# A two-layer streaming encoder step on one core: queue loads held behind older stores, weight splits at one step each, a first tile outside the pinned order, and all eight late key projections beside the first attention

## The chip, the cores and the metric

The kernel runs on one core of one Trainium2 chip. The time is the device time in microseconds (us) of one execution. The core's engines are named as the profile names them: PE (TensorE, matrix products; PEld is its weight load), DVE (VectorE), ACT (ScalarE), POOL (GpSimd) and SP (SyncE, which here only issues DMAs, one after the other). Each engine works through its own instructions in order and waits on semaphores for the others. Three runs of the kernel before took 3301.7, 3307.01 and 3307.56 us, a median of 3307.01 us.

## The reference

One step of a two-layer encoder over 2048 prompt frames and 64 sample frames, 16 heads of 64. Layer A is a softmax attention over a band of chunks, layer B a stick-breaking attention over all earlier frames; both multiply their output by a SiLU gate, project it and add it to the residual stream. Cut to what is computed:

```
def gated_out(o, gate, w_out):
    return (o.reshape(b, t, D_MODEL) * jax.nn.silu(gate)) @ w_out

def band_attend(q, k, v, q_pos, k_pos, rel_bias):            # layer A
    s = jnp.einsum('bqhd,bkhd->bhqk', q, k) * SCALE + rel_bias[:, rel]
    p = jax.nn.softmax(jnp.where(mask, s, NEG_INF), axis=-1)
    return jnp.einsum('bhqk,bkhd->bqhd', p, v)

def sb_block(q, k, v, q_pos, k_pos):                         # layer B
    z = jnp.einsum('bqhd,bkhd->bhqk', q, k) * SCALE
    log_fail = jnp.where(mask, jax.nn.log_sigmoid(-z), 0.0)
    later = jnp.flip(jnp.cumsum(jnp.flip(log_fail, -1), axis=-1), -1) - log_fail
    w = jnp.where(mask, jnp.exp(jax.nn.log_sigmoid(z) + later), 0.0)
    return jnp.einsum('bhqk,bkhd->bqhd', w, v)

layer A:  q, k, v, gate = split(rms_norm(x, norm_a) @ w_in_a);  x += gated_out(band(q, k, v), gate, w_out_a)
shared:   k, v = split(rms_norm(x, norm_kv) @ w_kv)
layer B:  q, gate = split(rms_norm(x, norm_b) @ w_in_b);        x += gated_out(sb(q, k, v), gate, w_out_b)
out:      rms_norm(x, norm_f), and the new rows of k and v of both layers
```

## The kernel before, in words

**Precision and products.** Every float32 operand is split into a high and a low part (`split`: ACT copies the rounded high part, DVE subtracts to get the low part), and a projection adds three products of such parts (`mm3`). The columns of one such product are 512, 364 or 362.

**Four stages stand one behind the other.** (1) `projections("a")`: the input rows are normed, turned by PE and split (`turned`, `parted`); the values of all heads are projected (`ps_v`); then the keys, queries and gates are projected pair of heads by pair of heads (`hp`, eight pairs), each in two halves of the frames. The first half is held in tiles `x_own`, the second in `big`; the products are written to `ps_t`. Beside it, stage functions prepare caches, biases and value differences (`stage_cache` with the flips `ps_c` on PE, `stage_bias`, `stage_diff`). All results go to scratch memory in HBM. (2) The band attention of layer A. (3) `projections("b")`, of the same build. (4) The stick-breaking attention of layer B.

**An attention is driven by `Beat`.** Each beat puts one score tile on PE (`z`), then turns weights that are a few beats old (`wt`), splits them (`ph`, `pl`) and multiplies them with the values (`acc`). Two groups of 512 queries stand in a part; ORDER takes groups 1 and 0 for all eight pairs, then 3 and 2. Beside the beats, `beat.beside` holds a list of jobs that are done in steps: `rate` (0.4 steps a beat in A, 0.3 in B) is added to `due`, and a step that has a product takes 1.0 from it, a step without one 0.5 (`return 1.0 if product else 0.5`, line 906). The jobs are, in order: late projections of the second half of the frames (`late_job`, products `ps_j` of six matmuls a step, eight steps a job; the list DEFER says which kinds and pairs), then eight steps that load the output weights (`woraw`) and split them into `big` (`w_out_steps`; no product), and once a group of queries is summed, the output projection of its token tiles (`out_tile`, products `ps_o`, eight steps a tile). In `lead`, 8 (A) or 14 (B) steps run ahead of the first beat. What is left at the end is done in a tail without beats.

**The order on SP.** All engines' instructions within an attention are pinned in program order by `order.on`; the loads and stores of `nc.sync` are not. Where these stand is decided by the scheduler that builds the program: a load may be put ahead of stores that were written down earlier, if its tile is free. SP then issues strictly in that order, and a DMA that waits for its data or its tile holds up all that stand behind it.

**Small tiles that are waited for.** The late jobs and the output tiles share few buffers: the outputs `sp` (a split key or query chunk), `sg` (a gate chunk), `lkn` (keys turned back to rows), `vcur` and `xr` all have the tag "xr" with two buffers, so the third of them waits until the store of the first has landed. `lkn` is written by POOL (`add_back`) and turned by PE (`token_rows`, `ps_r`).

**The first tile of `projections`.** `order.on = True` (line 274) is set before the first row tile is loaded, normed (ACT `junk`, DVE `ms`, POOL `rstd`, DVE `xt`) and turned, so all of that stands, on each engine, behind what was written down before it.

Of the kernel before, what the change touches and what calls it, by code (L numbers as in the profile page):

```python
# [16 lines left out]
P = 128  # L17
# [3 lines left out]
DH = 64  # L21
NP = 2048
NS = 64
# [17 lines left out]

DEFER = dict(a=[("k", hp) for hp in (4, 5, 6, 7)], b=[(k, hp) for k in "gq" for hp in range(HP)])

# [56 lines left out]
def encoder_step(ctx: ExitStack, tc: tile.TileContext, a: dict, o: dict):  # L100
# [14 lines left out]

    sp = order.engine(nc.sync)

    cpool = ctx.enter_context(tc.tile_pool(name="consts", bufs=1))
# [86 lines left out]

    def put(L, kind, hp, s, cols, part):

        for i in (0, 2) if kind == "q" and s == 0 else (s,):
            nc.sync.dma_start(f32(lay[L][kind][hp][i, :, cols]), f32(part))


    def projections(L, x_of, begin, w_v, cv, gv, out_v, jobs, first, prompt, sample, stages):
        with (
# [7 lines left out]
            with tc.tile_pool(name=f"v_{L}", bufs=2) as pool:  # L221

                x_new = []

                def turned(t, scale=gps.tensor_scalar):
                    r0, n = TOK[t]
                    xt = pool.tile([P, D], F32, name="xt", tag="xt", bufs=4)
                    nc.sync.dma_start(xt[:n], x_of(t))
                    junk = pool.tile([P, D], mybir.dt.bfloat16, name="junk", tag="junk", bufs=1)
                    r = rstd_of(pool, xt, n, junk)  # L230
                    scale(xt[:n], xt[:n], r[:n], 1.0, ALU.mult, ALU.mult)
                    halves = []
# [243 lines left out]
    def load_q(L, pool, hp, h, q0):  # L476

        there(L, "q", hp, q0)
        q = pool.tile([P, 2, CH], F32R, name="q", tag="q", bufs=3 if L == "a" else 2)
        src = f32(lay[L]["q"][hp][:, h * DH : h * DH + DH, place(q0) : place(q0) + CH]).rearrange("s d t -> d s t")  # L480
        for s in range(2):
            nc.sync.dma_start(f32(q[s * DH : s * DH + DH]), src[:, s : s + 2])
        return q

    def load_gate(L, pool, hp, q0):
        there(L, "g", hp, q0)
        gt = pool.tile([P, CH], F32, name="gt", tag="gt", bufs=2)
        nc.sync.dma_start(gt, lay[L]["g"][hp][:, place(q0) : place(q0) + CH])
        return gt

    def load_k(L, hp, k0, kt):

        there(L, "k", hp, k0)
        c = place(k0) if k0 < T else k0
        for s in range(2):
            src = f32(lay[L]["k"][hp][s, :, c : c + kt.shape[2]])
            nc.sync.dma_start(f32(kt[s * DH : s * DH + DH]), src.rearrange("(h d) t -> d h t", h=2))

    def load_v(L, pool, hp, k0, n, bufs):

        tag = "vn" if n == P else "vs" if bufs == 1 else "vt"
        vt = pool.tile([P, n // P, 2, P], F32R, name="vt", tag=tag, bufs=2 if n == P else bufs)
        nc.sync.dma_start(
            f32(vt), f32(lay[L]["v"][k0 : k0 + n, 2 * hp : 2 * hp + 2]).rearrange("(j p) h c -> p j h c", p=P)
        )
        return vt
# [6 lines left out]
    class Sample:  # L513
# [9 lines left out]
        def queries(self, hp):  # L523
            q = self.q[hp % 3]
            for h in range(2):
                rows = slice(h * DH, h * DH + DH)
                src = f32(lay[self.L]["q"][hp][0:2, rows, NEW : NEW + NS])
                nc.sync.dma_start(f32(q[rows, :, rows]), src.rearrange("s d t -> d s t"))
            return q

        def gate(self, pool, hp):
            gt = pool.tile([P, NS], F32, name="gs", tag="gs", bufs=2)
            nc.sync.dma_start(gt, lay[self.L]["g"][hp][:, NEW : NEW + NS])
            return gt

        def keys_values(self, pool, hp, k0, n, bufs):
            kt = pool.tile([P, 2, n], F32R, name="kt", tag="kn" if n == NS else "kt", bufs=2 if n == NS else bufs)
            c = place(k0) if k0 < T else k0
            nc.sync.dma_start(f32(kt), f32(lay[self.L]["k"][hp][:, :, c : c + n]).rearrange("s p t -> p s t"))

# [15 lines left out]
    def gate_steps(L, pool, acc, h, c0, n, gt, sums, hp, g):  # L556
# [12 lines left out]
        def close():  # L569
# [120 lines left out]
    def late_job(L, kind, w, c0, g, hp, x2, first, prompt):  # L690
# [23 lines left out]
        def out(c):  # L714
            ps = st["ps"]
            at = slice(place(HALF + c), place(HALF + c) + CH)
            if kind == "g":
                sg = opool.tile([P, CH], F32, name="sg", tag="xr", bufs=2)
                act.activation(sg, ps, AF.Sigmoid)
                dve.tensor_tensor(sg, ps, sg, ALU.mult)  # L720
                nc.sync.dma_start(lay[L]["g"][hp][:, at], sg)
            else:
                sp = opool.tile([P, 2, CH], F32R, name="sp", tag="xr", bufs=2)
                split(sp[:, 0], sp[:, 1], ps)
                for s in range(2):
                    put(L, kind, hp, s, at, sp[:, s])
                st[c] = sp
# [8 lines left out]
        def token_rows(c):  # L736
# [6 lines left out]
            dst = prompt[b : b + CH, hp * P : hp * P + P]  # L743
            nc.sync.dma_start(dst.rearrange("(j p) c -> p j c", p=P), kn[:, 1].rearrange("p (j c) -> p j c", j=4))

# [94 lines left out]
    class Beat:  # L840
# [3 lines left out]

        def __init__(self, lag, hold, scores_first):
            self.lag, self.hold, self.scores_first = lag, hold, scores_first
            self.clock = 0
# [15 lines left out]
        def step(self):  # L863
# [40 lines left out]
            if self.at == n:  # L904
                self.now = None
            return 1.0 if product else 0.5

# [16 lines left out]
        def beat(self, first=None):  # L924
# [43 lines left out]
        def end(self):  # L968
            self.rate = 1.0
            while self.tiles or self.blocks or self.held or self.marks:  # L970
                self.beat()
            order.amid = False
            while self.now or self.beside:
                self.ready = 0
# [48 lines left out]
    with (  # L1023
# [14 lines left out]
        def done_a(t, n, xr, c):  # L1038
            if c:
                nc.sync.dma_start(x1_rows(t), xr[:n])  # L1040

# [20 lines left out]
        def items():  # L1062
            for part in ORDER:
                for hp in range(HP):
                    c0, vs = max(min(part) - 1, 0), {}
                    keys = pool.tile([P, 2, SEEN * CH], F32R, name="keys", tag="keys", bufs=2)
                    for g in part:
                        sums = {}
                        for h in range(2):
# [4 lines left out]
                            if h == 0 and g == part[0]:  # L1074
                                bias = pool.tile([P, 2, 640], F32, name="bias", tag="bias", bufs=2)
                                nc.sync.dma_start(bias, biasd[hp])
                            for c in fresh:
# [51 lines left out]
        def sample_item(hp):  # L1129
            st, sums = {}, {}  # L1130

            def one():

                bs = pool.tile([P, 576], F32, name="bs", tag="bs", bufs=1)
                for h in range(2):
                    nc.sync.dma_start(bs[h * DH : h * DH + DH], biasd[hp][0:DH, h, 0:576])
                q = new.queries(hp)
# [61 lines left out]
    with (  # L1199
# [281 lines left out]
```

## Time and profile before

| what | value |
|---|---|
| median of 3 runs | 3307.01 us (3301.7 to 3307.56) |
| profiled execution, its own time | 3303.79 us |
| span of that execution's instructions | 3301.9 us |
| PE / DVE / ACT / POOL busy | 97% / 58% / 52% / 39% of the span |
| mean granted TensorE clock | 0.992 |
| data moved by DMA | 644.37 MB, 195 GB/s over the span |

The profile comes from one execution. Its tables give the busy time of each engine in chosen stretches of the span, the granted clock of TensorE in them (1.00 is full speed), and the mean busy share of the 16 DMA engines. A timeline row gives start, duration, engine, instruction, and in brackets the idle time ahead of it and what ended that. In names such as `ps_r<-ident,lkn`, the tile left of the arrow is written and those right of it are read; buffer numbers are left out. Nearly all compute instructions carry line 89, that of the recording helper, so tiles tell them apart.

### The profile page before, as it was taken

The numbers are of one execution on the slowest core, as the hardware profiler recorded it, in microseconds if no ns is written. First come the engines' busy times: TensorE is split into PE (matmuls) and PEld (weight loads), VectorE is DVE, ScalarE is ACT, GpSimd is POOL, SyncE is SP. The second block draws the span as 40 slices with busy tenths as digits, with TensorE's granted clock in tenths as the row PEclk, the third lists the DMA queues.
The fourth block names the chain that finished last, engine by engine and source line by source line (L and its number), as shares of the span: only waits on it lengthen the run. The fifth ranks groups of instructions, "written<-read, shape, count | busy, mean of one in ns | idle before, by whom it ended". The sixth has DMA issues, their size and how long they took to land.

```text
span 3301.9 us, 53682 instructions
## 1 busy us (share of the span) xinstructions
PE 3215.2 (97%) x17928; PEld 2796.8 (85%) x17928; DVE 1922.0 (58%) x3882; ACT 1730.6 (52%) x3815; POOL 1296.1 (39%) x1950
## 2 busy tenths in 40 slices
PE   9999999999999999999999999999999999999999
PEld 7889999988888898878889999788878877888877
DVE  4234431117787777232044333899888888888873
ACT  5223322227897777143133432666666666666662
POOL 3001120005575554021044200444467776777761
PEclk9999999999899999999999999999999999999999
DMA  6359994258889894554399857777634564455423
GB/s 205 115 197 348 343 342 144 91 172 257 238 244 246 228 256 139 171 169 140 105 352 354 287 186 224 204 204 195 192 103 132 155 190 132 123 149 142 131 82 118
DMA packets 459195, 644.37 MB, mean 195 GB/s; under 512 B 49845, under 2 KB 272085, under 8 KB 458918
## 3 DMA queue, kind: packets, MB, share of 16 engines
q1 hardware_dynamic: 399462, 589.80, 57.9%
q10 hardware_dynamic: 59456, 51.13, 4.8%
q8 instruction: 143, 2.34, 0.3%
q14 instruction: 134, 1.10, 0.1%
HBM read 389.90 MB, written 250.90 MB: 194 GB/s over the span
## 4 chain that ended last, share of the span: by engine, by line
PE 77%; DVE 8%; issue 5%; DMA 4%; ACT 3%; POOL 2%; SPq 1%; POOLq 0%; DVEq 0%; ACTq 0%
PE ps_t L89 25%; PE ps_v L89 11%; PE acc L89 10%; PE ps_o L89 8%; PE z L89 8%; PE wt L89 8%; PE ps_j L89 5%; DVE s L89 3%; DVE pl L89 2%; PE ps_tr L89 1%; DVE lwl L89 1%; ACT ph L89 1%; ACT s L89 1%; POOL s L89 1%; PE ps_c L89 1%
## 5 line engine op out<-in xcount | busy, mean ns | idle before, releaser
L89 DVE TENSOR_TENSOR pl<-wt,ph 128x512 fp32r<-128x512 f32 (+1 forms) x864 | 549.5, 653 | 104.3 <-ACT ph L89 101.4
L89 ACT ACTIVATE ph<-wt 128x512 fp32r<-128x512 f32 (+1 forms) x864 | 483.2, 577 | 200.4 <-PE wt L89 191.3
L89 PE MATMUL ps_t<-x_own,wh 128*128 128x362 f32 (+1 forms) x2304 | 569.2, 327 | 0.0
L89 PE MATMUL wt<-ident,s 128*128 128x128 f32 x3472 | 551.7, 276 | 9.5 <-DVE pl L89 6.1
L89 PEld LDWEIGHTS wt<-ident,s 128*128 128x128 f32 x3472 | 421.7, 142 | 84.1 <-DVE pl L89 10.1
L89 ACT ACTIVATE f<-z 128x512 f32<-128x512 f32 (+4 forms) x680 | 355.8, 536 | 191.0 <-PE z L89 123.4
L89 POOL TENSOR_TENSOR s<-f,s 128x256 f32<-128x256 f32 x416 | 358.6, 864 | 125.7 <-DVE s L89 118.0
L89 PEld LDWEIGHTS ps_t<-x_own,wh 128*128 128x128 f32 x2304 | 405.2, 188 | 2.2
L89 PE MATMUL acc<-ph,vt 128*128 128x512 f32 (+3 forms) x1088 | 376.5, 381 | 11.4 <-ACT ph L89 5.7
L89 PE MATMUL acc<-pl,vt 128*128 128x512 f32 (+3 forms) x1088 | 367.1, 371 | 19.3 <-DVE pl L89 18.2
L89 PE MATMUL z<-kt,q 128*128 128x512 f32 (+3 forms) x1280 | 371.7, 378 | 9.6 <-ACT f L89 9.2
L89 PE MATMUL ps_t<-x_own,wl 128*128 128x362 f32 (+1 forms) x1152 | 376.6, 327 | 0.0
L89 POOL TENSOR_SCALAR s<-s,rc 128x640 f32<-128x640 f32 (+5 forms) x264 | 194.8, 744 | 427.8 <-DMA keys<-k_a 250.7
L89 PE MATMUL ps_o<-big,oh 128*128 128x512 f32 x1088 | 337.9, 394 | 0.8 <-ACT oh L89 0.5
L89 DVE TENSOR_TENSOR_SCAN s<-two,s,own 128x256 f32<-128x256 f32 x408 | 298.6, 736 | 37.8 <-POOL two L89 28.4
L89 POOL TENSOR_TENSOR two<-f 128x256 f32<-128x256 f32 x416 | 261.9, 632 | 119.6 <-ACT f L89 108.6
L89 PE MATMUL ps_t<-big,wh 128*128 128x512 f32 x896 | 278.4, 391 | 0.0
L89 PEld LDWEIGHTS z<-kt,q 128*128 128x128 f32 x1280 | 221.4, 190 | 39.9 <-ACT f L89 16.7
L89 PEld LDWEIGHTS acc<-pl,vt 128*128 128x128 f32 x1088 | 196.1, 192 | 58.8 <-DVE pl L89 44.1
L89 PEld LDWEIGHTS ps_o<-big,oh 128*128 128x128 f32 x1088 | 203.0, 189 | 42.9 <-ACT oh L89 0.9
L89 PEld LDWEIGHTS acc<-ph,vt 128*128 128x128 f32 x1088 | 198.9, 192 | 35.5 <-ACT ph L89 11.5
L89 PEld LDWEIGHTS ps_t<-x_own,wl 128*128 128x128 f32 x1152 | 216.3, 188 | 0.1
(148 smaller groups left out, 5585.0 us busy)
## 6 DMA issues: line engine op xcount, KB each, us to landing
vt<-v_b SPq DMA_DIRECT2D x80, 512.0 KB, 4.9
v_b<-vs SPq DMA_DIRECT2D x64, 512.0 KB, 5.5
q<-q_a SPq DMA_DIRECT2D x128, 256.0 KB, 5.8
q<-q_b SPq DMA_DIRECT2D x128, 256.0 KB, 4.2
vt<-v_a SPq DMA_DIRECT2D x48, 512.0 KB, 7.6
kt<-k_b SPq DMA_DIRECT2D x96, 256.0 KB, 6.2
keys<-k_a SPq DMA_DIRECT2D x80, 256.0 KB, 6.9
v_a<-vs ACTq DMA_DIRECT2D x32, 512.0 KB, 2.6
```

The source lines that it names most:

```text
L89: ins = op(*args, **kwargs)
```

## The change

The change has five parts. (a) DEFER of layer A names the keys of all eight pairs, not of four: the second half of the keys of pairs 0 to 3 leaves `projections("a")` and becomes four more late jobs at the head of the list. (b) A class `Queue` notes the stores of the two attentions with the beat at which they are written down; a load that is written down 24 or more beats after a store gets an order edge, so that it stands behind that store on SP. There is no wait in it, only a place. (c) A step without a product takes 1.0 instead of 0.5 from `due`. (d) In `projections("b")` the first tile's load and norm are written down ahead of `order.on = True`, so the scheduler may place them. (e) The pass-through of stores and loads to `queue`. Core of the diff:

```
-DEFER = dict(a=[("k", hp) for hp in (4, 5, 6, 7)], b=[(k, hp) for k in "gq" for hp in range(HP)])
+DEFER = dict(a=[("k", hp) for hp in range(HP)], b=[(k, hp) for k in "gq" for hp in range(HP)])
...
+    class Queue:
+        def __init__(self, pace):
+            self.pace, self.clock, self.stores = pace, 0, []
+        def store(self, out, in_):
+            self.stores.append((self.clock, nc.sync.dma_start(out, in_)))
+        def load(self, out, in_):
+            while len(self.stores) > 1 and self.stores[1][0] <= self.clock - self.pace:
+                self.stores.pop(0)
+            behind = self.stores and self.stores[0][0] <= self.clock - self.pace
+            with tc.issue_after(self.stores[0][1].ins) if behind else nullcontext():
+                nc.sync.dma_start(out, in_)
+        def clear(self):
+            self.clock, self.stores = 0, []
+    queue = Queue(24)
...
-                def turned(t, scale=gps.tensor_scalar):
+                def normed(t, scale=gps.tensor_scalar):
...
+                    return xt
+                def turned(t, scale=gps.tensor_scalar, xt=None):
+                    r0, n = TOK[t]
+                    if xt is None:
+                        xt = normed(t, scale)
...
+                        xt0 = normed(seq[0], dve.tensor_scalar) if L == "b" else None
                         order.on = True
-                        tile0 = turned(seq[0], dve.tensor_scalar)
+                        tile0 = turned(seq[0], dve.tensor_scalar, xt0)
...
-            nc.sync.dma_start(f32(q[s * DH : s * DH + DH]), src[:, s : s + 2])
+            queue.load(f32(q[s * DH : s * DH + DH]), src[:, s : s + 2])
...
-            nc.sync.dma_start(lay[L]["o"][g][hp], ot[:, :n])
+            queue.store(lay[L]["o"][g][hp], ot[:, :n])
...
-            return 1.0 if product else 0.5
+            return 1.0 if product else self.blank
...
             self.clock += 1
+            queue.clock = self.clock
...
-        beat = Beat(LAG["a"], HOLD["a"], True)
+        beat = Beat(LAG["a"], HOLD["a"], True, 1.0)
...
-        beat = Beat(LAG["b"], HOLD["b"], False)
+        beat = Beat(LAG["b"], HOLD["b"], False, 1.0)
```

The other loads of the two attentions (keys, values, gates, biases, the sample's) go through `queue.load` in the same way, and the stores of late jobs, attention outputs and layer A's rows through `queue.store`.

How the instructions stand now. First place: SP, where the first attention begins. The names `q`, `keys`, `bias`, `vt`, `gt` are loads of the first pairs; `bs`, `gs`, `kt` and the `vt` after them are loads of the sample's attention, which is computed in the second part; `k_a...<-sp` are the stores of the first late key job (its first chunk is `sp_6177` before and `sp_5905` after). Before:

```order
L503 DMA vt_6659<-v_a_97 128x4x256
L488 DMA gt_6694<-gate_a0_98 128x512
L1136 DMA bs_10430<-bias_0_143 64x576 x2
L533 DMA gs_10435<-gate_a0_98 128x64
L539 DMA kt_10437<-k_a0_89 128x2x512
L209 DMA k_a4_93<-sp_6177 128x512
L503 DMA vt_10439<-v_a_97 128x4x256
L209 DMA k_a4_93<-sp_6177 128x512
L539 DMA kt_10441<-k_a0_89 128x2x64
L503 DMA vt_10443<-v_a_97 128x256
```

The same place on SP of the changed kernel:

```order
L132 DMA vt_6385<-v_a_97 128x4x256
L399 DMA gate_a7_105<-sg_5766 128x1024
L132 DMA vt_6387<-v_a_97 128x4x256
L132 DMA gt_6422<-gate_a0_98 128x512
L125 DMA k_a0_89<-sp_5905 128x512 x2
L125 DMA k_a0_89<-sp_5986 128x512 x2
L132 DMA q_6251<-q_a0_81 64x2x512 x2
L89 DMA lraw_6033<-in_w_in_a 128x8x128
```

The sample's loads are gone from here, and the four stores of the first late job stand behind the first pairs' loads directly. From the first load of this attention (before, three small `qs` loads of the sample ahead of it) to the first chunk's second store there are 34 DMAs before and 26 now.

Second place: SP, where the second attention begins, from the first to the second store of the first late gate job (`gate_b0...<-sg`). Before:

```order
L721 DMA gate_b0_128<-sg_21229 128x512
L482 DMA q_21414<-q_b0_111 64x2x512 x2
L488 DMA gt_21683<-gate_b0_128 128x512
L539 DMA kt_21778<-k_b0_119 128x2x64
L503 DMA vt_21780<-v_b_127 128x256
L539 DMA kt_21802<-k_b0_119 128x2x512
L503 DMA vt_21804<-v_b_127 128x4x256
L497 DMA kt_21820<-k_b1_120 64x2x512 x2
L721 DMA gate_b0_128<-sg_21258 128x512
```

In the changed kernel:

```order
L125 DMA gate_b0_128<-sg_21313 128x512
L132 DMA q_21498<-q_b0_111 64x2x512 x2
L132 DMA gt_21767<-gate_b0_128 128x512
L125 DMA gate_b0_128<-sg_21342 128x512
L125 DMA q_b0_111<-sp_21405 128x512 x3
```

Nine DMAs stood between the two stores, and three do now.

Third place: ACT, at the end of the first layer's tail, where the first tile of the second layer is normed (`junk<-xt`); `oh<-og` are the splits of the tail's output tiles, `vwh` those of the next weights. Before:

```order
L89 ACTIVATE oh_15527<-og_15523 128x4x64 x2
L89 ACTIVATE oh_15588<-og_15584 128x512 x2
L89 ACTIVATE ol_15528<-ps_o_15579 64x512
L89 ACTIVATE ol_15528<-ps_o_15605 64x512
L89 ACTIVATE junk_15702,ss_15703<-xt_15700 128x1024
L89 ACTIVATE vwh_15722<-vraw_15720,g_kv_79 128x512
```

In the changed kernel:

```order
L89 ACTIVATE oh_14955<-og_14951 128x512 x2
L89 ACTIVATE oh_15107<-og_15103 128x512 x2
L89 ACTIVATE junk_15786,ss_15787<-xt_15784 128x1024
L89 ACTIVATE oh_15170<-og_15166 128x512 x2
L89 ACTIVATE oh_15233<-og_15229 128x512 x2
```

The norm of the first tile now stands ahead of the splits of the tail's last nine output tiles; its DVE parts (`ms`, `xt`) have moved with it.

On PE the number of instructions is the same; 192 products of 512 columns go from `ps_t` to `ps_j`. In the first attention, the score tiles that stand on PE between the last `ps_j` and the first `ps_o`, with no product beside them, were 88 and are 30. In the second, that distance was 26 and is 39. Behind the last score tile of the first attention stood 512 `ps_o` products, and 560 stand there now.

More of the change, by code (lines that the diff above doesn't have):

```diff
@@ L204, in mm3, with put @@
             mm(out, sl(k), mh(k), start=False, stop=(k == NK - 1))
-    def put(L, kind, hp, s, cols, part):
+    def put(L, kind, hp, s, cols, part, by=nc.sync.dma_start):
         for i in (0, 2) if kind == "q" and s == 0 else (s,):
-            nc.sync.dma_start(f32(lay[L][kind][hp][i, :, cols]), f32(part))
+            by(f32(lay[L][kind][hp][i, :, cols]), f32(part))
     def projections(L, x_of, begin, w_v, cv, gv, out_v, jobs, first, prompt, sample, stages):
@@ L487, in load_gate @@
         gt = pool.tile([P, CH], F32, name="gt", tag="gt", bufs=2)
-        nc.sync.dma_start(gt, lay[L]["g"][hp][:, place(q0) : place(q0) + CH])
+        queue.load(gt, lay[L]["g"][hp][:, place(q0) : place(q0) + CH])
         return gt
@@ L496, in load_k @@
             src = f32(lay[L]["k"][hp][s, :, c : c + kt.shape[2]])
-            nc.sync.dma_start(f32(kt[s * DH : s * DH + DH]), src.rearrange("(h d) t -> d h t", h=2))
+            queue.load(f32(kt[s * DH : s * DH + DH]), src.rearrange("(h d) t -> d h t", h=2))
     def load_v(L, pool, hp, k0, n, bufs):
@@ L502, in load_v @@
         vt = pool.tile([P, n // P, 2, P], F32R, name="vt", tag=tag, bufs=2 if n == P else bufs)
-        nc.sync.dma_start(
+        queue.load(
             f32(vt), f32(lay[L]["v"][k0 : k0 + n, 2 * hp : 2 * hp + 2]).rearrange("(j p) h c -> p j h c", p=P)
@@ L527, in queries @@
                 src = f32(lay[self.L]["q"][hp][0:2, rows, NEW : NEW + NS])
-                nc.sync.dma_start(f32(q[rows, :, rows]), src.rearrange("s d t -> d s t"))
+                queue.load(f32(q[rows, :, rows]), src.rearrange("s d t -> d s t"))
             return q
@@ L532, in gate @@
             gt = pool.tile([P, NS], F32, name="gs", tag="gs", bufs=2)
-            nc.sync.dma_start(gt, lay[self.L]["g"][hp][:, NEW : NEW + NS])
+            queue.load(gt, lay[self.L]["g"][hp][:, NEW : NEW + NS])
             return gt
@@ L538, in keys_values @@
             c = place(k0) if k0 < T else k0
-            nc.sync.dma_start(f32(kt), f32(lay[self.L]["k"][hp][:, :, c : c + n]).rearrange("s p t -> p s t"))
+            queue.load(f32(kt), f32(lay[self.L]["k"][hp][:, :, c : c + n]).rearrange("s p t -> p s t"))
             r0, m = (k0 - NS * (self.L == "b"), P) if n == NS else (k0, n)
@@ L720, in out @@
                 dve.tensor_tensor(sg, ps, sg, ALU.mult)
-                nc.sync.dma_start(lay[L]["g"][hp][:, at], sg)
+                queue.store(lay[L]["g"][hp][:, at], sg)
             else:
@@ L725, in out @@
                 for s in range(2):
-                    put(L, kind, hp, s, at, sp[:, s])
+                    put(L, kind, hp, s, at, sp[:, s], queue.store)
                 st[c] = sp
@@ L743, in token_rows @@
             dst = prompt[b : b + CH, hp * P : hp * P + P]
-            nc.sync.dma_start(dst.rearrange("(j p) c -> p j c", p=P), kn[:, 1].rearrange("p (j c) -> p j c", j=4))
+            queue.store(dst.rearrange("(j p) c -> p j c", p=P), kn[:, 1].rearrange("p (j c) -> p j c", j=4))
         chunks = range(0, HALF, CH)
@@ L840, in encoder_step, with __init__ @@
     class Beat:
-        def __init__(self, lag, hold, scores_first):
-            self.lag, self.hold, self.scores_first = lag, hold, scores_first
+        def __init__(self, lag, hold, scores_first, blank):
+            self.lag, self.hold, self.scores_first, self.blank = lag, hold, scores_first, blank
             self.clock = 0
@@ L972, in end @@
             order.amid = False
+            queue.clear()
             while self.now or self.beside:
@@ L1039, in done_a @@
             if c:
-                nc.sync.dma_start(x1_rows(t), xr[:n])
+                queue.store(x1_rows(t), xr[:n])
         def soft_max(b, out, z, s):
@@ L1075, in items @@
                                 bias = pool.tile([P, 2, 640], F32, name="bias", tag="bias", bufs=2)
-                                nc.sync.dma_start(bias, biasd[hp])
+                                queue.load(bias, biasd[hp])
                             for c in fresh:
@@ L1135, in one @@
                 for h in range(2):
-                    nc.sync.dma_start(bs[h * DH : h * DH + DH], biasd[hp][0:DH, h, 0:576])
+                    queue.load(bs[h * DH : h * DH + DH], biasd[hp][0:DH, h, 0:576])
                 q = new.queries(hp)
```

## The prediction

> **What bounds the kernel now.** I read the page's first two parts, then busy time by stage, then the waits inside the stages that lose time.
>
> ```profile
> span 3301.9 us, 53682 instructions
> PE 3215.2 (97%) x17928; PEld 2796.8 (85%) x17928; DVE 1922.0 (58%) x3882; ACT 1730.6 (52%) x3815; POOL 1296.1 (39%) x1950
> PE 77%; DVE 8%; issue 5%; DMA 4%; ACT 3%; POOL 2%; SPq 1%; POOLq 0%; DVEq 0%; ACTq 0%
> ```
>
> PE is the bound: it is busy for 97% of the span and carries 77% of the chain that ended last. PE's number of instructions does not change, so the change can win only what PE loses: idle time, and time at a lowered clock. By stages (start and end, length, busy us of each engine with the number of instructions, granted clock, DMA share, GB/s):
>
> ```profile
> core 0: us, PE busy (x) PEld busy (x) DVE busy (x) ACT busy (x) POOL busy (x), PEclk, DMA share, GB/s
> 213.00:352.00 139.00, 137.93 (x783) 129.24 (x782) 68.57 (x178) 52.57 (x140) 22.33 (x24) 1.00 0.94 327
> 744.00:768.00 24.00, 18.54 (x100) 16.30 (x100) 14.11 (x48) 15.49 (x42) 9.31 (x14) 0.79 0.99 293
> 768.00:870.00 102.00, 100.13 (x621) 89.65 (x621) 75.09 (x220) 82.26 (x197) 60.09 (x72) 0.98 0.83 239
> 870.00:912.00 42.00, 34.18 (x196) 30.40 (x196) 35.62 (x96) 36.86 (x84) 22.64 (x25) 0.84 0.86 244
> 912.00:1008.00 96.00, 90.23 (x610) 81.41 (x608) 80.16 (x244) 91.40 (x215) 71.65 (x87) 0.98 0.91 249
> 1320.00:1428.00 108.00, 108.00 (x490) 89.80 (x489) 29.14 (x48) 17.67 (x34) 3.24 (x3) 1.00 0.50 161
> 1428.00:1440.00 12.00, 9.41 (x42) 7.06 (x41) 8.09 (x14) 7.15 (x14) 3.25 (x5) 0.86 0.65 218
> 2056.00:2072.00 16.00, 10.63 (x50) 8.75 (x49) 9.33 (x16) 6.91 (x17) 5.83 (x11) 0.79 1.04 286
> 2700.00:2736.00 36.00, 28.46 (x153) 20.88 (x152) 34.86 (x56) 24.74 (x52) 26.61 (x40) 1.00 0.81 261
> ```
>
> I price a stretch as its length less PE's busy time, plus its length times what the clock lacks to 1.00. So 744 to 768 (start of the first attention) loses 5.5 + 0.21 x 24 = 10.5 us; 870 to 912 (the output weights' splits) 7.8 + 6.7 = 14.5; 912 to 1008 5.8 + 1.9 = 7.7; 1428 to 1440 (first tile of the second layer) 2.6 + 1.7 = 4.3; 2056 to 2072 (start of the second attention) 5.4 + 3.4 = 8.7; 2700 to 2736 (second output weights) 7.5. The first layer's tail, 1320 to 1428, loses nothing, so products moved into it cost their plain time.
>
> **Start of the first attention: -9 us.**
>
> ```profile
> 756.11 1.11 PE L89 MATMUL ps_r<-ident,lkn 128*128 128x128 f32 x4 [4.71 <-POOL lkn L89]
> 714.99 1.99 SPq L528 DMA_DIRECT2D qs<-q_a  x3
> 742.12 1.11 SPq L1136 DMA_DIRECT2D bs<-bias  x2
> 748.64 0.32 SPq L209 DMA_DIRECT2D k_a<-sp  x1
> 748.64 6.02 DMA k_a<-sp
> ```
>
> PE waits 4.71 us for `lkn`, whose buffer comes free when the first chunk's second store has landed: issued at 748.64, landed 6.02 later at 754.66. That store was the 34th DMA from 714.99, so SP took (748.64 - 714.99) / 33 = 1.02 us for each. The order now has 26. Eight fewer put the store at 740.5 and its landing at 746.5, ahead of PE, which began to wait at 751.4. Stall and clock loss together are 10.5; I leave 1.5 for smaller waits. Bounds: 0, if something else holds SP up, and -10.5.
>
> **Start of the second attention: -7.5 us.**
>
> ```profile
> 2066.11 1.22 PE L89 MATMUL z<-kt,q 128*128 128x512 f32 x2 [5.34 <-ACT f L89]
> 2064.97 0.60 ACT L89 ACTIVATE sp<-ps_j 128x512 fp32r<-128x512 f32 x1 [5.30 <-DMA gate_b<-sg]
> 2044.20 2.31 SPq L721 DMA_DIRECT2D gate_b<-sg  x1
> 2056.86 0.34 SPq L721 DMA_DIRECT2D gate_b<-sg  x1
> ```
>
> ACT is stuck at `sp` until the second gate store has landed, and the scores `f` behind it keep PE. Between the two stores stood nine DMAs, and three do now; at the pace between these rows, 12.66 / 10 = 1.27 us, the second store is issued 7.6 us earlier, more than ACT's 5.30 us. Of 8.7 I take 7.5. Bounds 0 and -8.7.
>
> **First tile of the second layer: -3 us.**
>
> ```profile
> 1432.16 1.09 PE L89 MATMUL ps_tr<-ident,xt 128*128 128x128 f32 x8 [2.37 <-issue]
> 1429.83 0.69 DVE L89 TENSOR_TENSOR xr<-ps_o,xr 128x512 f32<-128x512 f32 x1 [4.75 <-PE ps_o L89]
> 1431.30 0.75 DVE L89 TENSOR_SCALAR xt<-xt,rstd 128x1024 f32<-128x1024 f32 x1 [0.72 <-POOL rstd L89]
> 1432.82 1.08 ACT L89 ACTIVATE x_own<-ps_tr 128x512 fp32r<-128x512 f32 x2 [8.92 <-PE ps_tr L89]
> ```
>
> The norm stood behind the tail's last addition on DVE, and PE waited 2.37 us. It now lies in the tail, where DVE and ACT are mostly free (29.14 and 17.67 of 108 us). What is late next is `x_own`, 1.08 us on ACT, so of 4.3 some 1.3 stays. Bounds 0 and -4.3.
>
> **Middle of the first attention: -6 us.** The 88 score tiles without a product beside them become 30, now all in the second part, with the 16 split halves among them. Rows of such a stretch, two items in each window, and of the splits:
>
> ```profile
> 912.00:924.00 12.00, 10.94 (x73) 9.30 (x72) 9.39 (x34) 11.89 (x31) 11.08 (x15) 1.00 0.91 257
> ...
> sum 48.00, PE 42.26 PEld 36.22 DVE 36.56 ACT 45.69 POOL 42.49; mean PE 10.57 PEld 9.06 DVE 9.14 ACT 11.42 POOL 10.62
> L89 ACT ACTIVATE big<-woraw 128x512 fp32r<-128x512 f32 x32 | 18.3, 626 | 6.9 <-DMA woraw<-in_w_out_b 5.0 <-DMA woraw<-in_w_out_a 1.9
> L89 DVE TENSOR_TENSOR big<-woraw,big 128x512 fp32r<-128x512 f32 x32 | 25.1, 818 | 3.1 <-ACT big L89 3.0
> ```
>
> The sum is of four windows (912, 936, 960 and 984, 12 us each) over the wide tiles, which have no product beside them: there ACT is 95% busy and PE idle for 5.74 of 48 us, 12%. At 96 / 64 = 1.5 us a tile (sixteen items of four tiles in 912 to 1008), 30 tiles take 45 us and lose 5.4. The splits ask ACT for 16 x 18.3 / 32 = 9.2 us, and ACT's 5% of 45 us absorb 2.2, so 7 more are lost. The other 58 tiles get products; at the 768 to 870 row's loss (1.9 + 2.0 of 102) on about 58 x 2 us that is 4.5. Together 17 instead of 14.5 + 7.7 = 22.2: I take -6, rounded up for the loads of `woraw` that now have twice the beats to land. Bounds: -15 if the splits hide in gaps (22.2 less 5.4 and a 1.9 of idle), and +7 if the 0.84 clock of 870 to 912 holds for the 45 us.
>
> **Second output weights: -1.5 us.**
>
> ```profile
> 2701.38 9.79 DMA woraw<-in_w_out_b
> 3120.00:3168.00 48.00, 46.14 (x260) 35.85 (x258) 43.69 (x71) 34.20 (x69) 40.09 (x79) 1.00 0.25 71
> ```
>
> The stretch grows from 26 to 39 tiles. The late load of 9.79 us gets more time, but the last row, a stretch without products, has DVE at 91%: in 39 x 1.5 = 58 us it has 5.2 us to spare for 25.1 / 2 = 12.6 us of splits. So most of the 7.5 stays. Bounds -6 and +3.
>
> **The moved products: +3 us.** 192 products leave the key projections, where PE ran without a gap.
>
> ```profile
> 1329.75 100.06 PE ps_o L89 x441
> ```
>
> At 100.06 / 441 = 0.227 us they take 43.6 us off that stage and put the same into the attention, of which 48 output products pass on to the tail. As PE time this is nothing. But the 139 us from 213 to 352 moved 139 x 327 = 45.5 MB at a DMA share of 0.94, and shrink to 95.4 us. Four pairs' stores of 0.5 + 0.5 MB and four row stores of 0.25 MB go away, 5 MB, and 40.5 MB remain, 124 us at that rate. Most of it (biases, value differences) is no input of PE there, and lies before a stage with a share of 0.58 at 352 to 725, so it can run on. I take 3 us, between 0 and 28.
>
> ```profile
> 352.00:725.00 373.00, 373.00 (x1994) 342.24 (x1993) 88.40 (x220) 97.58 (x243) 28.90 (x23) 1.00 0.58 208
> ```
>
> The four jobs also load and split their weights again: 32 `lwh` and `lwl` more, about 0.4 us each on ACT and DVE, under products of PE. The order edge itself is no wait: the store named is at least 24 beats old, some 24 x 1.5 = 36 us. What it holds back is the sample's loads; were the first of them late, PE would wait at most one landing of its 512 KB keys, once in each attention.
>
> ```profile
> kt<-k_a SPq DMA_DIRECT2D x8, 512.0 KB, 7.4
> ```
>
> So 0 to 7.4 us; I take 0, since the sample is computed over a hundred beats after the start and its loads are still free to go 24 beats ahead.
>
> The sum is -9 - 7.5 - 3 - 6 - 1.5 + 3 = -24 us: 3303.8 - 24 = 3279.8, predicted 3280. The profiled execution lies 3.2 us below the median of 3307.01, inside the spread of the three runs.
>
> [...] The windows show the clock falling after short gaps: 0.86 in 1428 to 1440, where the longest gap is 2.37 us. [...]
>
> **Rivals.**
> - *The starts keep their stalls.* The stores move up on SP, but SP then waits for their data, or the DMA share of 0.99 and 1.04 there lengthens the landing. Without the two starts' 16.5 us: 3296. Against it: 8.2 and 7.6 us of lead for stalls of 4.7 and 5.3.
> - *The splits vanish in the gaps.* Both weights' splits reach their lower bounds and the moved products cost nothing: -9 - 7.5 - 3 - 15 - 6 = -40.5, 3263. For it: ACT and DVE were at 88% and 85% in 870 to 912, so waiting, not work, set that loss. Against it: ACT's 95%.
> - *Nothing is gained on balance.* The scheduler's order differs nearly everywhere on SP; new waits of the old sizes (10.5, 8.7) appear elsewhere and eat the 24 us less a few: 3302.
> - *Slower: the shortened key stage is bound by DMA.* PE turns eight cached key blocks (`ps_c`) there in order, each behind a load in SP's line. If all 40.5 MB must land, PE waits 28 us, 3.5 at each, and at half clock for some 3.4 us after each (as 1.7 of 12 us went at 1428), 14 more: -27 + 28 + 14 = +15, 3319. It decides from a wait of 1.7 us at each: 8 x (1.7 + 1.7) is the gain of 27. Against it: before, PE lost only 1.07 us in that stage.
>
> **How the numbers follow.** The forecast (3268 to 3290) has 0.55, the kept stalls 0.17, the hidden splits 0.13, no balance 0.08, the DMA-bound stage 0.07. The first three are faster by over 0.2% (6.6 us, about what a measurement can tell from no change): 0.85. The range from 3257 to 3304 leaves out the slower rival and a little below the hidden splits.
>
> **What would show it.** Right: `ps_r` near the first attention's start waits under 1 us; the second attention's start has a clock of 1.00; about 1 us ahead of the first `ps_v` of the second layer; 30 tiles in the middle with PE at 70 to 80% and ACT above 95%. Wrong: PE waits for `kr` or `ps_c` ahead of 310 us, or a clock below 0.9 in a stretch where it was 1.00.

## The result, and the profile after

The changed kernel takes 3313.38 us (median of 8 runs, 3307.84 to 3320.69); the kernel before, run beside it, 3305.88 us (8 runs, 3300.29 to 3307.64). The ratio of the two sets of runs is 1.0028, 95% interval 1.0019 to 1.0038 (the two medians alone give 1.0023): slower by 0.28%. The prediction was 3280 us, faster. The profiled execution took 3312.76 us; its page, with the group of the score products of the second attention:

```profile
span 3310.8 us, 53792 instructions
...
PE 3215.5 (97%) x17928; PEld 2790.9 (84%) x17928; DVE 1933.0 (58%) x3914; ACT 1744.2 (53%) x3847; POOL 1303.8 (39%) x1950
...
L89 PE MATMUL z<-kt,q 128*128 128x512 f32 (+3 forms) x1280 | 372.8, 379 | 25.1 <-DMA q<-q_b 20.9
```

PE is busy for the same time as before, 3215 us. The last line holds the news: PE stood idle for 20.9 us ahead of score products because query loads had not landed. Where along the span the loss sits is read from the first and the last start of three tiles, here the rows of the changed kernel for the first tile of the second layer (`ps_tr`), the scores of the second attention (`z`) and its late products (`ps_j`), each with the first and last start in us:

```profile
L89 PE MATMUL ps_tr<-ident,xt x136: 221/272/329, 1415.0 to 1510.5; 128*128 128x128 f32 x128, 64*128 64x64 f32 x8
...
L89 PE MATMUL z<-kt,q x1280: 219/392/793, 2033.6 to 3192.7; 128*128 128x512 f32 x123, 128*128 128x128 f32 x25, 128*128 128x384 f32 x25, 128*128 128x256 f32 x10
...
L89 PE MATMUL ps_j<-big,lwl x256: 387/390/628, 2016.9 to 2690.1; 128*128 128x512 f32 x128
```

The same three rows of before:

```profile
L89 PE MATMUL ps_tr<-ident,xt x136: 221/272/328, 1432.2 to 1527.6; 128*128 128x128 f32 x128, 64*128 64x64 f32 x8
L89 PE MATMUL z<-kt,q x1280: 220/392/792, 2051.3 to 3183.9; 128*128 128x512 f32 x123, 128*128 128x128 f32 x25, 128*128 128x384 f32 x25, 128*128 128x256 f32 x10
L89 PE MATMUL ps_j<-big,lwl x256: 387/391/486, 2034.6 to 2683.4; 128*128 128x512 f32 x128
```

From these starts and the two spans:

| stretch | before, us | after, us |
|---|---|---|
| start to the first `ps_tr` of the second layer (the first layer) | 1432.2 | 1415.0 |
| from there to the first score of the second attention | 619.1 | 618.6 |
| from there to its last late product | 632.1 | 656.5 |
| from there to the end | 618.5 | 620.7 |

In this execution the first layer gives 17.2 us, the second layer's projections give 0.5, the first half of the second attention (from its first score to its last late product) takes 24.4 back, and the rest takes 2.2. The stretches that answer to those shown of before (columns as there):

```profile
213.00:308.00 95.00, 94.35 (x587) 93.92 (x587) 49.97 (x149) 42.65 (x121) 8.80 (x13) 1.00 0.97 326
684.00:712.00 28.00, 25.27 (x141) 22.01 (x140) 15.42 (x48) 15.82 (x36) 8.81 (x12) 0.94 0.90 279
838.00:984.00 146.00, 142.55 (x895) 126.13 (x893) 109.98 (x313) 118.79 (x283) 84.76 (x101) 1.00 0.87 249
984.00:1066.00 82.00, 75.63 (x500) 67.28 (x499) 71.00 (x176) 72.19 (x157) 48.62 (x52) 1.00 0.99 272
1409.00:1421.00 12.00, 11.45 (x51) 8.35 (x50) 6.46 (x11) 5.56 (x10) 1.65 (x2) 1.00 0.62 194
2040.00:2056.00 16.00, 13.09 (x69) 9.13 (x67) 15.59 (x27) 12.55 (x30) 9.28 (x19) 1.00 0.99 276
2296.00:2378.00 82.00, 67.07 (x377) 57.19 (x377) 61.72 (x110) 45.28 (x105) 32.45 (x54) 0.89 0.73 177
2706.00:2742.00 36.00, 29.13 (x165) 22.91 (x165) 33.59 (x55) 26.76 (x54) 27.56 (x45) 0.95 0.83 254
```

The shortened key stage (213 to 308) still keeps PE busy for 94.35 of 95 us. The start of the first attention (684 to 712) loses 2.7 + 0.06 x 28 = 4.4 us where 10.5 were lost; its middle (838 to 1066) loses 3.5 + 6.4 = 9.8 where 870 to 1008 lost 22.2; the first tile (1409 to 1421) 0.6 where 4.3 were lost; the start of the second attention (2040 to 2056) 2.9 where 8.7 were lost, though a wait of 2.82 us for a query load follows at 2058. Then 2296 to 2378, a stretch that no term of the prediction named: 14.9 us idle and 0.11 x 82 = 9.0 us of clock, 24 us in 82. Its DMA share is 0.73, so the DMA engines are not full; something is late.

The chain that ended last, followed back through the first of the two long stalls there (start, duration, what):

```profile
2302.74 13.92 DMA kt<-k_b
2316.66 0.02 issue
2316.68 7.19 DMA q<-q_b
2323.87 0.14 issue
2324.01 0.66 PE z L89 x2
```

A key load takes 13.92 us to land, SP issues the query load at the end of the chain only when it has, and that takes another 7.19 us, while PE waits. What SP issued in the 19 us ahead of it (start, time on SP, DMA):

```profile
2297.76 0.59 SPq L132 DMA_DIRECT2D kt<-k_b  x1
2298.39 0.47 SPq L132 DMA_DIRECT2D vt<-v_b  x1
2298.90 0.43 SPq L132 DMA_DIRECT2D kt<-k_b  x1
2299.38 0.47 SPq L132 DMA_DIRECT2D vt<-v_b  x1
2299.89 1.33 SPq L132 DMA_DIRECT2D kt<-k_b  x2
2301.32 0.66 SPq L132 DMA_DIRECT2D vt<-v_b  x1
2302.03 1.33 SPq L132 DMA_DIRECT2D kt<-k_b  x2
2303.46 0.53 SPq L132 DMA_DIRECT2D vt<-v_b  x1
2304.82 0.34 SPq L125 DMA_DIRECT2D o_b<-ot  x1
2307.70 0.33 SPq L132 DMA_DIRECT2D gt<-gate_b  x1
2309.20 5.03 SPq L125 DMA_DIRECT2D q_b<-sp  x3
2315.99 3.35 SPq L132 DMA_DIRECT2D q<-q_b  x4
```

All keys and values of a pair, ten loads, go out within 6.3 us (2297.76 to 2304.0), one behind the other, then SP slows down, and the next queries stand at the end of the line. That is the picture the theory starts from.

### The profile page after: what moved, and what is told of

It is laid out like the page before. It is cut to its first block, busy times and chain, and to the rows that moved or that the text cites. A ratio compares the mean times of both kernels' runs of the same rounds, so it can differ in the third digit from the quotient of the medians.

```text
span 3310.8 us, 53792 instructions
## 1 busy us (share of the span) xinstructions
PE 3215.5 (97%) x17928; PEld 2790.9 (84%) x17928; DVE 1933.0 (58%) x3914; ACT 1744.2 (53%) x3847; POOL 1303.8 (39%) x1950
## 4 chain that ended last, share of the span: by engine, by line
PE 74%; issue 8%; DVE 8%; DMA 5%; ACT 3%; SPq 1%; POOL 1%; POOLq 0%; DVEq 0%; ACTq 0%
PE ps_t L89 24%; PE ps_v L89 11%; PE acc L89 9%; PE z L89 8%; PE wt L89 8%; PE ps_j L89 6%; PE ps_o L89 5%; DVE s L89 3%; DVE pl L89 3%; DMA q<-q_b 1%; DMA kt<-k_b 1%; SPq L132 1%; PE ps_tr L89 1%; ACT ph L89 1%; DMA vt<-v_b 1%
## 5 line engine op out<-in xcount | busy, mean ns | idle before, releaser
L89 PE MATMUL z<-kt,q 128*128 128x512 f32 (+3 forms) x1280 | 372.8, 379 | 25.1 <-DMA q<-q_b 20.9
L89 PE MATMUL ps_j<-big,lwh 128*128 128x512 f32 x768 | 250.0, 402 | 0.8 <-ACT lwh L89 0.3
L89 PE MATMUL ps_t<-big,wh 128*128 128x512 f32 x768 | 238.8, 391 | 0.0
L89 DVE TENSOR_TENSOR_SCAN s<-f,own 128x128 f32<-128x128 f32 (+4 forms) x264 | 201.9, 787 | 47.7 <-ACT f L89 38.4
```

The source lines that it names most:

```text
L89: ins = op(*args, **kwargs)
```

## The experiments

**Theory H:** the order edge does it. All loads of a pair are written down within a few beats, so they name the same store as the one to stand behind; none may go ahead of it, and behind it they all come at once. **Rival C:** the products' cadence does it (blank steps, those without a product, at 1.0 in the second attention; the expectations call them "blank scores").

The edits of the first four, each against the changed kernel:

```
e1   beat = Beat(LAG["b"], ...)          followed by   queue.pace = 10**9
e2   -    queue = Queue(24)                            + queue = Queue(10**9)
e3   as the kernel before, with the class Queue, and a pace of 24 in the second attention only
e4   -    queue = Queue(24)                            + queue = Queue(48)
```

Held in the first attention only, and not at all:

> The changed kernel with loads held in the first attention only; in the second they are issued as in the kernel before. Theory H (the hold keeps each pair's key and value loads back until they come in one run, up to 1728 KB between two engine waits of SP's order against 1024 KB without it, and the query loads of the next tile stand behind that run): the 20.9 us that PE waited for q<-q_b in the second attention and most of the 23.8 us at half clock beside them go, the second attention's start stall of the kernel before (5.3 us, plus half clock) may come back: 3285 to 3295 us, PE waits for q<-q_b under 3 us. Rival C (the cadence of the products: blank scores of the second attention cost 1.0 in place of 0.5, so that scores and products meet other loads): the waits for q<-q_b stay, 3310 to 3316 us.

> The changed kernel with no load held in either attention. Theory H: as e1 in the second attention. In the first attention it tells what took the start stall of the kernel before (4.7 us, 10.2 us at half clock) away: if the hold did, the stall is back and the time is 8 to 12 us above e1; if the keys of eight pairs did, it is within 3 us of e1. Rival C: 3310 to 3316 us.

The kernel before with the hold in the second attention, and a longer pace:

> The kernel before with one thing added: loads of the second attention are held (24 beats); keys of four pairs, blank scores at 0.5 and the first tile as before. Theory H: PE waits 15 to 25 us for q<-q_b in the second attention, and the time is 3318 to 3330 us. Rival C: the products' order is nearly that of the kernel before, so 3303 to 3309 us.

> The changed kernel with a pace of 48 beats in place of 24 in both attentions: a load is held only behind a store that is 48 beats old. Theory H: the longest run of loads in the second attention's SP order is 1024 KB again, as without a hold, so the waits for q<-q_b go and the time is within 4 us of e1. Rival C: 3310 to 3316 us. If any hold at all costs in the second attention, whatever its pace, 3300 to 3313 us.

| run | median, us | ratio to before | 95% interval | first layer, us | second attention, first half, us |
|---|---|---|---|---|---|
| before | 3305.21 | | | 1432.2 | 632.1 |
| changed kernel | 3313.38 | 1.0028 | 1.0019 to 1.0038 | 1415.0 | 656.5 |
| e1 held in the first attention only | 3295.41 | 0.9968 | 0.9959 to 0.9978 | 1423.8 | 631.2 |
| e2 not held | 3293.19 | 0.9969 | 0.9958 to 0.9980 | 1420.9 | 631.9 |
| e3 before, held in the second | 3328.14 | 1.0068 | 1.0051 to 1.0085 | 1437.6 | 646.8 |
| e4 pace 48 | 3294.94 | 0.9969 | 0.9957 to 0.9981 | 1419.1 | 630.6 |

The last two columns are read from one trace of each as above; each ratio is to the runs of before beside it (the changed kernel's had 3305.88 us). Theory H holds, rival C falls: without the hold in the second attention the changed kernel is faster than before by 0.3%, the hold alone makes the kernel before slower by 0.7%, and the products' cadence is that of the changed kernel in e1, e2 and e4. In these three no PE wait for `q<-q_b` is left among the waits of 2030 to 2720. In e3 that wait is 14.7 us, just under the 15 to 25 expected, and e1's time lies 0.4 us above its range; the other times of this set are as theory H had them. Of e3's 22.3 us in the trace, 17.4 lie in the second attention; the other 5 lie in stages ahead of it, which have no hold in either kernel. At the place of the listing above, e1's SP issued this:

```profile
2305.35 0.37 SPq L132 DMA_DIRECT2D vt<-v_b  x1
2306.45 0.32 SPq L125 DMA_DIRECT2D o_b<-ot  x1
2306.83 0.42 SPq L132 DMA_DIRECT2D gt<-gate_b  x1
2308.69 0.37 SPq L132 DMA_DIRECT2D kt<-k_b  x1
2309.16 3.28 SPq L125 DMA_DIRECT2D q_b<-sp  x3
2313.62 6.76 SPq L132 DMA_DIRECT2D q<-q_b  x4
```

The same gate, store and query DMAs, but one key and one value load among them: the others had gone out earlier and apart, five keys in a row from 2288.06 us and three values from 2300.64. The landing times say the same, from the trace's DMA groups for 2030 to 2700 (KB each, median us to landing), first the changed kernel:

```profile
q<-q_b SPq DMA_DIRECT2D x89, 256.0 KB, 4.3
vt<-v_b SPq DMA_DIRECT2D x43, 512.0 KB, 8.7
```

and e1:

```profile
vt<-v_b SPq DMA_DIRECT2D x50, 512.0 KB, 4.3
q<-q_b SPq DMA_DIRECT2D x90, 256.0 KB, 4.2
```

Values take twice as long to land in the kernel with the long rows. The medians of the keys go both ways (256 KB: 7.3 us in the changed kernel, 6.4 in e1; 512 KB: 4.6 and 6.7). A typical query load takes no longer, which is why no median of `q` shows it; the six that PE waited for landed 6.6 to 9.0 us after their issue.

e1 and e2 differ in the first attention's hold alone, and do not differ in time. The stall at its start is there without the hold (e2) and smaller with it (e1), where another tile is waited for. The PE row of e2, and that of e1 (start, duration, in brackets the idle time ahead and what ended it):

```profile
710.53 1.12 PE L89 MATMUL ps_r<-ident,lkn 128*128 128x128 f32 x4 [5.92 <-POOL lkn L89]
```

```profile
703.12 0.69 PE L89 MATMUL wt<-ident,s 128*128 128x128 f32 x2 [3.84 <-POOL s L89]
```

So the hold shortens that stall by 2 us in these traces, and the time shows nothing of it; the two intervals leave room for a gain of up to some 5 us, and none for the 8 to 12 us that the expectation named.

**Which loads?** The second set tells theory K (the row of keys and values is what costs) from rival Q (the query loads are late because they are held themselves), asks how the cost depends on the pace, and takes the moved keys alone:

```
e5   in the second attention load_q, load_gate, Sample.queries, Sample.gate:
     -  queue.load(...)      + nc.sync.dma_start(...)
e6   in the second attention load_k, load_v, Sample.keys_values:
     -  queue.load(...)      + nc.sync.dma_start(...)
e7   beat = Beat(LAG["b"], ...)          followed by   queue.pace = 36
e8   the kernel before with
     -DEFER = dict(a=[("k", hp) for hp in (4, 5, 6, 7)], ...
     +DEFER = dict(a=[("k", hp) for hp in range(HP)], ...
```

> The changed kernel, but in the second attention only the loads of keys and values are held; query and gate loads are issued freely (the first attention is as in the changed kernel). Theory K (what costs is the run of held key and value loads: it fills the queue, and whatever stands behind it lands late): runs of up to 2048 KB remain, so PE waits 8 to 25 us for q<-q_b and the time is 3303 to 3320 us. Rival Q (what costs is that the query loads themselves are held behind a store and so are issued late): waits under 4 us, 3289 to 3299 us.

> The counterpart: in the second attention only query and gate loads are held; keys and values are issued freely. Theory K: the longest run is 1024 KB as without a hold, waits for q<-q_b under 4 us, 3287 to 3298 us. Rival Q: waits of 8 to 25 us, 3303 to 3320 us.

> The changed kernel with a pace of 36 beats in the second attention (24 in the first, as in the changed kernel): the longest runs of loads are 1312 to 1376 KB, between the 1728 KB of pace 24 and the 1024 KB without a hold. Theory K, if the cost grows with the run: 3296 to 3308 us, waits for q<-q_b of 3 to 14 us. If there is a length up to which a run costs nothing, and 1376 KB lies under it: 3290 to 3297 us, waits under 3 us.

> The kernel before with one thing added: the second half's keys of all eight pairs are projected beside the first attention (no hold, blank scores at 0.5, first tile as before). If the gain in the first layer is from the keys alone: 3294 to 3299 us (the 10 to 12 us of the runs without a hold, less about 4 us for the first tile of the second layer, where the gap of 2.4 us and 3.4 us at half clock stays). If the products' cadence (blank scores at 1.0) is needed for it: 3301 to 3308 us.

| run | median, us | ratio to before | 95% interval | first layer, us | second attention, first half, us |
|---|---|---|---|---|---|
| before | 3303.66 | | | | |
| e5 keys and values held | 3308.44 | 1.0013 | 1.0002 to 1.0025 | 1421.7 | 650.5 |
| e6 queries and gates held | 3293.97 | 0.9973 | 0.9964 to 0.9983 | 1419.7 | 631.6 |
| e7 pace 36 | 3293.46 | 0.9970 | 0.9960 to 0.9980 | 1428.2 | 630.4 |
| e8 before, keys of eight pairs | 3310.55 | 1.0021 | 1.0013 to 1.0030 | 1439.1 | 631.4 |

K holds, Q falls as the main cause: with free query loads (e5) PE waits for them all the same, behind held keys and values. The PE waits of e5 in 2030 to 2720 (total, times, longest):

```profile
PE z L89 <- DMA q<-q_b: 16.1, 5, 5.8
```

With held query loads and free keys and values (e6) that wait is not there, and nothing is lost.

At a pace of 36 (e7) the cost is gone (630.4 us), as in the second branch of its expectation. Counted in the traces, from 2060 to 2450 us, the longest row of key and value loads with no other DMA of SP between them is ten in the changed kernel and in e3, eight in e5, and four or five in before and in all other runs, e7 (four) among them. The traces with the long rows are the ones that lose time there, and e5, with shorter rows than the changed kernel, waits less (16.1 against 20.9 us). By this count e7 does not lie between 24 and 48, as its expectation had it by the KB between two of SP's waits, so it doesn't tell how the cost grows between a row of five and one of eight. Why 36 beats make no long rows was not tested.

e8 was a miss on both counts: the keys alone were to bring 5 to 10 us or, if they needed the cadence, to end at 3301 to 3308 us; at 3310.55 they cost 7. Where the time goes, the ACT rows of e8 in 700 to 1300 and the busy times of 65 us in its middle show:

```profile
L89 ACT ACTIVATE big<-woraw 128x512 fp32r<-128x512 f32 x16 | 9.3, 624 | 7.3 <-DMA woraw<-in_w_out_a 7.3
```

```profile
980.00:1045.00 65.00, 50.50 (x303) 44.38 (x301) 49.46 (x114) 48.82 (x104) 31.36 (x32) 0.89 0.82 239
```

ACT stands in order behind a weight row that has not landed, and `ph` behind it keeps PE: 14.5 us idle and 7.2 us of clock. A step without a product costs 0.5 here, so the splits follow each other twice as fast as at 1.0, and each weight row has half the beats to land. That is about the loss that before has beside its splits (22.2 us), so it has not gone; why e8 is 7 us slower than before, these rows don't show. The last set sorts cadence, first tile and the start:

```
e9   in Queue.load: self.pace = 24 if self.clock < self.until else 48
     in the second attention: queue.until = 40  (elsewhere 24 throughout)
e10  the kernel before with xt0 = normed(...) ahead of order.on = True
e11  e8 with Beat(LAG["a"], HOLD["a"], True, 1.0)
e12  the kernel before with blank steps at 1.0 in both attentions
```

> The changed kernel with two paces in the second attention: loads are held behind stores of 24 beats for its first 40 beats, and of 48 beats behind that. SP's order then has the changed kernel's start (3 DMAs between the two gate stores) and no run of loads over 1024 KB. If the start stall (3.9 us and 6.8 us at half clock with a pace of 48 throughout) goes with the order at the start alone: 5 to 8 us under the kernel with pace 48, 3286 to 3291 us, and no wait for q<-q_b over 3 us. Rival (the stall is only put off, as any hold at the start makes a later load late): 3292 to 3298 us.

> The kernel before with the second layer's first tile loaded and normed before the hand-written order begins, and nothing else. The gap of 2.4 us and half of the 3.4 us at half clock behind it go: 3298 to 3302 us where the kernel before measures 3304. Rival (the products behind only wait for the next tile instead): 3303 to 3306 us.

> The kernel before with the keys of all eight pairs moved and blank scores at 1.0 in the first attention; no hold, the second attention's cadence at 0.5 and the first tile as before. If the keys need the slower cadence, and this alone turned their 7 us loss into the gain of the runs without a hold: 3293 to 3299 us. If the second attention's cadence had a part in that gain: 3300 to 3308 us.

> The kernel before with blank scores at 1.0 in both attentions, and nothing else: keys of four pairs, no hold, first tile as before. If keys and cadence add up (keys alone cost 7 us, both gain 6): 3288 to 3294 us. If the cadence only pays where eight pairs' products have to be spread (with four pairs the products of the first attention run out after 123 of its 565 us): 3300 to 3306 us.

| run | median, us | ratio to before | 95% interval | first layer, us | second attention, first half, us |
|---|---|---|---|---|---|
| before | 3303.57 | | | | |
| e9 two paces | 3292.11 | 0.9966 | 0.9954 to 0.9978 | 1424.6 | 629.7 |
| e10 first tile alone | 3301.31 | 0.9994 | 0.9985 to 1.0003 | 1427.6 | 632.1 |
| e11 keys and cadence | 3299.48 | 0.9985 | 0.9976 to 0.9994 | 1421.7 | 631.4 |
| e12 cadence alone | 3303.59 | 0.9996 | 0.9987 to 1.0004 | 1425.5 | 631.1 |

e11 turns e8 round: the same keys with steps at 1.0 are faster than before by 0.15% (3299.48 us, between the two ranges expected), and the same two views of it have no wait for `woraw` and a full clock:

```profile
L89 ACT ACTIVATE big<-woraw 128x512 fp32r<-128x512 f32 x16 | 9.3, 624 | 0.0
```

```profile
977.00:1042.00 65.00, 59.22 (x404) 52.59 (x403) 60.99 (x148) 61.88 (x133) 41.20 (x43) 1.00 1.03 286
```

The cadence alone (e12) cannot be told from no change, as was expected if it only pays where eight pairs' products have to be spread; keys and cadence belong together. The first tile alone (e10) takes the gap of 2.37 us ahead of the first `ps_tr` away. The way to that product is 4.6 us shorter in its trace, but before and e3, whose orders on PE and SP are the same up to there, differ by 5.4; its time, 2.3 us shorter, is not told from no change by its interval.

e9 has the changed kernel's order at the second attention's start and no long rows behind 2060 us. The stall on `f` of before (5.34 us) is gone from its trace, and this is late next:

```profile
2067.48 0.41 PE L89 MATMUL z<-kt,q 128*128 128x128 f32 x2 [1.75 <-DMA q<-q_b]
```

At 3292.11 us it has the lowest median of all, but its interval covers those of e1, e2, e4, e6 and e7: neither 3286 to 3291 nor the rival's 3292 to 3298 is shown. All six beat both kernels, each by its ratio to before, by more than the measurement is uncertain.

## Why the prediction was wrong

- **The step that failed is the order edge, costed at 0:** "The order edge itself is no wait: the store named is at least 24 beats old ... its loads are still free to go 24 beats ahead." Nothing waits at the edge, that is true. But the edge also takes away the lead that each load had when it was issued as its tile came free, and sets all loads of a pair in one place. I asked whether the *store* would be late, and whether one load would be; I did not count what the loads do to those behind them on SP. Price: 3313.4 against 3293 to 3295 us of e1, e2 and e4, which have no long rows of loads, 18 to 20 us, and 3328.1 against 3305.2, 23 us, on the kernel before (17 of them in the second attention of its trace). The bound of 0 to 7.4 us stood on one landing, where six stalls came, two of 6.61 and 7.16 us. That the hold of keys and values in the second attention costs this is shown by e1 to e6. Why longer paces cost nothing is not tested by itself; their traces have no long rows of loads.
- **Start of the first attention (-9):** right in kind. The stall on `lkn` is gone in the changed kernel, with 2.65 us on `s` next: 4.4 us lost instead of 10.5. But e1, with the same orders in this layer, waits 3.84 us on `s`, and e2 has the old stall on `lkn` and the same time as e1, so 9 us did not reach the end.
- **Middle of the first attention (-6):** right in sign, and twice as large in this trace: 22.2 us of loss became 9.8. The mis-sized term is the 7 us for the splits. Between the last late product and the first output product (971.6 to 1035.6 us) ACT is busy for 95%, as forecast, but PE for 90% with a full clock: 6.1 us lost, where 5.4 + 7 were expected. That is the rival of the splits that vanish in the gaps, in this layer. The reason given in passing, that `woraw` has twice the beats to land, is the one that e8 and e11 show; it deserved a term.
- **Moved products (+3):** too dear. The key stage shrank by 734.7 - 687.9 = 46.8 us from the start to the first score, and its DMA share of 0.97 at 326 GB/s cost PE nothing. The slower rival that I wrote down (PE waits at `ps_c`) did not come.
- **First tile (-3):** right in kind. The gap of 2.37 us stands in all five traces without this edit (before, e3, e8, e11, e12) and in none of the nine with it. The 1.7 us of clock behind it stand in only two of the five (before and e8), so a part of the term was luck of the trace that I read; the time of e10 does not tell the gain from none.
- **All of the first layer:** forecast -9 - 6 + 3 - 3 = -15. The changed kernel's trace has -17.2, but it was a lucky one: the same first layer, with the same orders on PE and SP, took 1415.0, 1423.8, 1421.7, 1419.7, 1428.2 and 1424.6 us in six traces (changed, e1, e5, e6, e7, e9), a mean of 1422.2, against 1432.2 and 1437.6 (before, e3), a mean of 1434.9. That is -12.7, with single traces 13 us apart.
- **Start of the second attention (-7.5):** mis-sized. Where its stall goes and the rows of loads too (e9), the first half is 2.4 us shorter than before (629.7 against 632.1): the query load is late next by 1.75 us, and the `ps_j` products behind it start 0.42 us apart, against 0.227 us for each `ps_o`, also of 512 columns, at a full clock in before. In the changed kernel the same place waits 2.82 us. My sum moved the stall and did not ask what would be late next.
- **Second output weights (-1.5):** wrong sign. From the last late product to the end, before, e8, e10 and e11 (steps at 0.5 there) take 618.5 to 619.5 us, the changed kernel and the eight others with steps at 1.0 take 619.3 to 622.0: some 2 us more (e3, with steps at 0.5 but held loads, has 621.2). The stretch from 2706 to 2742 lost 6.9 + 0.05 x 36 = 8.7 us where 7.5 were lost. The second attention as a whole takes 1250.6 us in before and 1250.2 to 1253.9 in the ten traces without long rows of loads: there start and weights together gained nothing.
- **The account:** -12.7 - 2.4 + 2 = -13 without the long rows of loads, near to the -11 us of e9's 0.9966, so some 11 us of the forecast's 24 were terms taken too large, and the rows of loads cost another 18 to 20. The 0.07 for slower went to a rival with another mechanism.

## What to carry to other kernels

An edge that only moves an instruction can have a price even if nothing ever waits at it, 18 to 23 us here: ask which transfers it lets loose together, and which small transfer that an engine waits for stands behind them in the same queue. When loads are held back, look at the time of each one's landing before and after, not at the age of what they are held behind. Two edits of one change can each look useless or harmful alone (keys +0.2%, cadence 0) and gain together, so undo parts from the whole as well as adding them one by one.

## What the runs showed of the hardware

In these traces stalls cost clock in steps, and short ones not every time. The granted clock of the changed kernel around its two long gaps, and around one of 2.23 us:

```profile
2316.00:2334.00 18.00, 11.39 (x50) 9.47 (x49) 7.18 (x14) 4.15 (x12) 0.86 (x1) 0.72 0.53 149
2366.00:2386.00 20.00, 12.84 (x58) 10.65 (x57) 7.16 (x14) 4.96 (x12) 0.87 (x1) 0.74 0.57 165
1294.00:1304.00 10.00, 7.77 (x32) 6.30 (x32) 3.63 (x8) 3.09 (x7) 0.32 (x1) 0.83 0.57 203
```

The gap of 2.23 us took 0.17 x 10 = 1.7 us of clock with it, those of 6.61 and 7.16 us 0.28 x 18 = 5.0 and 0.26 x 20 = 5.2, while the stretch from 984 to 1066, whose gaps are at most 1.24 us, has 1.00. So these stalls of some 7 us were worth 12. In windows of 1 us the clock of these stretches, and around the gaps of 2.37, 4.71 and 5.34 us of before, reads 1.00 or 0.50, but for the windows in which it changes; what it lacks to 1.00 sums to 1.71 us with the gaps of 2.23 and 2.37 us, to 3.42 with that of 5.34, and to 5.12 with those of 4.71, 6.61 and 7.16. So a gap of 2.2 to 2.4 us did cost clock, here and in the trace of before. But the gap of 2.23 us, the same to 0.01 us and ahead of the same product, stands in nine traces, and in the 10 us around it the clock is 0.83 in six of them (changed, e1, e4, e5, e7, e9) and 1.00 in three (e2, e6, e11). So a clock loss behind a gap of this size, read from one trace, is not yet a gain that an edit can count on; what decides it, the runs don't show.

The same first layer takes between 1415 and 1428 us in executions with the same orders on PE and SP. A difference of 10 us between two single traces of a stage says little until a second trace of each is beside it.
